# Four passes over blocks of 256 tokens become two passes over blocks of 512, with streamed weights

## The chip, the cores and the metric

The kernel runs on one core of a Trainium2 chip. The core has a TensorE (PE in the profile) with its own memory for sums (PSUM, eight banks of 512 fp32 columns), VectorE (DVE), ScalarE (ACT), GpSimd (POOL), and a sync engine (SP) whose queue issues nearly all DMA transfers here. Every engine takes its instructions in the order of its own queue and waits by semaphores for the others. The metric is the device time of one execution in microseconds; each time is the median of several runs.

## The reference

One layer on 2048 tokens of width 1024, fp32. One input projection gives sixteen groups of columns; three head groups work on them, and an output projection with a residual and a final RMSNorm ends the layer.

```python
hn = rmsnorm(x, norm_g)
z = jnp.einsum('bsd,de->bse', hn, w_in)
(aq, ak, av, ag, mq, mk, mv, mo, mi, mf, mg, gq, gk, gv, ga, gg) = jnp.split(z, split_idx, axis=-1)
y_a = band_chunk_attention(aq, ak, av, rel_bias) * jax.nn.silu(ag)
qk = jax.nn.silu(causal_conv(jnp.concatenate([mq, mk], axis=-1), conv_w))
h_ml = mlstm_chunkwise(mq_c, mk_c, mv, mi + b_i, mf + b_f)
y_b = jax.nn.sigmoid(mo) * head_rmsnorm(h_ml, ml_norm_g, ML_HEADS) * jax.nn.silu(mg)
h_gla = gla_chunkwise(gq, gk, gv, log_alpha)
y_c = head_rmsnorm(h_gla, gla_norm_g, GLA_HEADS) * jax.nn.silu(gg)
y = jnp.concatenate([y_a, y_b, y_c], axis=-1)
return rmsnorm(x + jnp.einsum('bse,ed->bsd', y, w_out), final_g)
```

Attention looks back 8 chunks of 64 tokens. mLSTM and GLA carry a state from chunk to chunk; both are computed in chunks of 128 or 64 tokens with a matrix inside the chunk and a state between chunks.

## The kernel before

Projections keep near fp32 precision in three matmuls: weights and activations are each split into a high and a low part of a rounded type (`load_w` L84, `load_x` L117), and `mm3` (L101 to L104) adds high x high, high x low and low x high over eight k tiles into one PSUM bank. `proj_f` gives [columns x tokens] with 256 tokens as the moving side; `proj_t` gives [tokens x columns] with up to 384 columns.

The tokens come in eight blocks of 256 (ST), and the program walks over them four times:

- Pass 1 (from L135): normalise a block (`prep` L171; the first block starts on unnormalised x, `first_step` L202), store the normalised block to DRAM (`x_d`, L195), the gates of mLSTM (`gates`), the projections mq, mk, mv with the causal convolution (`proj1` L306), and two chunks of 128 tokens of mLSTM (`mlstm` L361).
- Pass 2: reload the block from `x_d` and split it again (L123, L124), GLA with its projections (`proj2`, `gla`), and mLSTM's output gates (`proj_ml`).
- Pass 3: reload again, the projections of attention (`proj3` L696), scores and softmax (`scores`, L770 to L783), and the weighting of the values (`mix`, L805 to L827).
- Pass 4: output projection, residual and final norm (L843 on).

Each of the eleven tiles of input weights [1024 x 384] is loaded and split once. Between stages, results go through DRAM.

A chunk of mLSTM runs so. `gates` writes the rows of the stabiliser to DRAM (`nm_d` L293, `iw_d` L294). Four DMAs read them back, copied to all partitions (`nmb` L369, `iwb` L371). POOL adds the row term (L386) and masks (L387), ACT takes the exponential (L389), DVE multiplies by the scores (L392), TensorE sums over the chunk (L404) and updates the state (L410). For the head norm ACT squares (L422), DVE and POOL make a scale (L424 to L433), DVE applies it (L435), TensorE transposes (L440) and ACT writes out (L443, stored by L444).

The order on each engine is set when the program is built, by a scheduler that weighs the program's order, priorities and a model of the durations; pools of few buffers add waits. Once built, each engine's order is fixed.

Of the kernel before, what the change touches and what calls it, by code (L numbers as in the profile page):

```python
# [18 lines left out]
KT = D // P  # L19
ST = 256  # L20
L = 128
AH, MH, GH = 6, 6, 4
WT = 384
EPS = 1e-6
NEG = -1e30

# [6 lines left out]
def trunk_kernel(ctx: ExitStack, tc: tile.TileContext, xT, x, w_tiles, w_gates, w_out, norm_g, conv_w,  # L33
                 gate_sel, one_row, bias, ml_g, gla_g, final_g, out, dbg=None):
    nc = tc.nc
    S = x.shape[0]
    NS = S // ST
# [3 lines left out]
    wring = ctx.enter_context(tc.tile_pool(name="wring", bufs=4))  # L41
    raws = ctx.enter_context(tc.tile_pool(name="raws", bufs=3))
    xs = ctx.enter_context(tc.tile_pool(name="xs", bufs=2))
    zz = ctx.enter_context(tc.tile_pool(name="zz", bufs=2))
# [3 lines left out]
    def bank(tag):  # L48
        return ps_g.tile([P, 512], FP32, name=tag)

    x_d = dram.tile([NS, P, KT, ST], FP32, name="x_d")
    nm_d = dram.tile([MH, S], FP32, name="nm_d")
    iw_d = dram.tile([MH, S], FP32, name="iw_d")
    ls_d = dram.tile([P, S], FP32, name="ls_d")
    hb_d = dram.tile([P, 3, S], FP32, name="hb_d")
# [3 lines left out]
    y_d = dram.tile([NS, P, KT, ST], FP32, name="y_d")  # L59

    def z_tile(shape, dt=FP32):
        return zz.tile(shape, dt, name="z")

    def t_tile(shape, dt=FP32):
        return zz.tile(shape, dt, name="t", bufs=4)

    def u_tile(shape, dt=FP32):
        return zz.tile(shape, dt, name="u", bufs=3)
# [10 lines left out]
    ng = const.tile([P, KT], FP32, name="ng")  # L79
    cw = const.tile([P, 6, 4], FP32, name="cw")  # L80

    W = {}

    def load_w(name, src, width=WT, split=nc.gpsimd, pre=None, post=None):  # L84
        hi = wring.tile([P, KT, WT], FR, name="wh")
        lo = wring.tile([P, KT, WT], FR, name="wl")
        W[name] = (hi, lo)
        for g in range(4):
            if pre is not None:
                pre(g)  # L90
            raw = raws.tile([P, 2, WT], FP32, name="raw")
            nc.sync.dma_start(raw[:, :, :width], src[g])
            ks = slice(2 * g, 2 * g + 2)
            nc.scalar.copy(hi[:, ks, :width], raw[:, :, :width])
            split.tensor_tensor(lo[:, ks, :width], raw[:, :, :width], f32(hi[:, ks, :width]), op=ALU.subtract)  # L95
            if post is not None:
                post(g)

    def mm3(ps, kk, hi, lo, xh, xl, stat_w, first, last):
        a = (hi, lo) if stat_w else (xh, xl)  # L100
        b = (xh, xl) if stat_w else (hi, lo)  # L101
        nc.tensor.matmul(ps, a[0], b[0], start=first, stop=False)  # L102
        nc.tensor.matmul(ps, a[0], b[1], start=False, stop=False)  # L103
        nc.tensor.matmul(ps, a[1], b[0], start=False, stop=last)  # L104

    def proj_f(ps, wn, c0, X):
        hi, lo = W[wn]
        for k in range(KT):
            mm3(ps, k, hi[:, k, c0:c0 + P], lo[:, k, c0:c0 + P], X[:, k, 0, :], X[:, k, 1, :], True, k == 0, k == KT - 1)

    def proj_t(ps, wn, c0, n, X, tt):
        hi, lo = W[wn]
        t = slice(tt * P, (tt + 1) * P)
        for k in range(KT):
            mm3(ps, k, hi[:, k, c0:c0 + n], lo[:, k, c0:c0 + n], X[:, k, 0, t], X[:, k, 1, t], False, k == 0, k == KT - 1)

    def load_x(s, src, eng):  # L117
        X = xs.tile([P, KT, 2, ST], FR, name="x")
        for k0, kn in ((0, 3), (3, 3), (6, 2)):
            ks = slice(k0, k0 + kn)  # L120
            raw = raws.tile([P, 3, ST], FP32, name="raw")
            nc.sync.dma_start(raw[:, :kn], src[s, :, ks])
            nc.scalar.copy(X[:, ks, 0, :], raw[:, :kn])  # L123
            eng.tensor_tensor(X[:, ks, 1, :], raw[:, :kn], f32(X[:, ks, 0, :]), op=ALU.subtract)  # L124
        return X

    def store_y(s, k, t0, y):
        nc.sync.dma_start(y_d[s, :, k, t0:t0 + y.shape[-1]], y)

# [1 line left out]
    with ExitStack() as p1:  # L131
        big = p1.enter_context(tc.tile_pool(name="p1big", bufs=2))
        one = p1.enter_context(tc.tile_pool(name="p1one", bufs=1))

# [3 lines left out]
        rst = one.tile([MH, ST], FP32, name="rst")  # L138
        nc.vector.memset(rst, 1.0)
        for c in range(ST // L):  # L140
            nc.vector.memset(rst[:, c * L:c * L + 1], 0.0)
# [3 lines left out]
        mlg = one.tile([P, 3], FP32, name="mlg")  # L145

        def load_consts():
# [7 lines left out]
        def rstd(rb, rs):  # L155
            nc.gpsimd.tensor_tensor(rs, rs, mhalf[:, 0:2], op=ALU.pow)
            dg = one.tile([P, 2, P], FP32, name="dg", bufs=1)
            for tt in range(2):
                nc.vector.tensor_scalar(dg[:, tt, :], ident, rs[:, tt:tt + 1], None, op0=ALU.mult)
            nc.tensor.matmul(rb[:, 0:ST], ones, dg.rearrange("p a t -> p (a t)"), start=True, stop=True)  # L160

        def gate_rows(rows):
            gp = bank("w")
            for k in range(KT):
                nc.tensor.matmul(gp[32 * (k % 4):32 * (k % 4) + 32, :ST], wg[:, k, :], rows(k),
                                 start=(k < 4), stop=(k >= 4), skip_group_check=True)
            g1 = big.tile([P, ST], FP32, name="g1", bufs=1)
            nc.scalar.activation(g1, gp[:, :ST], AF.Identity, bias=onerow)
            return g1

        def prep(s):  # L171
            t0 = s * ST
            s4 = big.tile([P, 2, 2], FP32, name="s4")
            rs = big.tile([P, 2], FP32, name="rs")
            rb = bank("w")
            X = xs.tile([P, KT, 2, ST], FR, name="x")
            for tt in range(2):
                for g in range(2):
                    xt = big.tile([P, D // 2], FP32, name="xt")
                    nc.sync.dma_start(xt, x[t0 + tt * P:t0 + (tt + 1) * P, g * 512:(g + 1) * 512])  # L180
                    nc.scalar.activation(X[:, 2 * tt + g].rearrange("p l t -> p (l t)"), xt, AF.Square,
                                         accum_out=s4[:, tt, g:g + 1])
            nc.vector.tensor_tensor(rs, s4[:, :, 0], s4[:, :, 1], op=ALU.add)
            nc.vector.tensor_scalar(rs, rs, 1.0 / D, EPS, op0=ALU.mult, op1=ALU.add)
            rstd(rb, rs)
            rws = []
            for k0, kn in ((0, 3), (3, 3), (6, 2)):
                ks = slice(k0, k0 + kn)
                raw = raws.tile([P, 3, ST], FP32, name="raw")
                rws.append(raw)  # L190
                nc.sync.dma_start(raw[:, :kn], xT[:, ks, t0:t0 + ST])
                for k in range(kn):
                    nc.vector.scalar_tensor_tensor(raw[:, k, :], raw[:, k, :], ng[:, k0 + k:k0 + k + 1], rb[:, :ST],
                                                   op0=ALU.mult, op1=ALU.mult)
                nc.sync.dma_start(x_d[s, :, ks], raw[:, :kn])  # L195
                nc.scalar.copy(X[:, ks, 0, :], raw[:, :kn])
                nc.gpsimd.tensor_tensor(X[:, ks, 1, :], raw[:, :kn], f32(X[:, ks, 0, :]), op=ALU.subtract)  # L197
            g1 = gate_rows(lambda k: rws[k // 3][:, k % 3, :])
            return X, g1

        # the first step's projections start on unnormalised x, scaled as they leave PSUM
        def first_step():  # L202
            za = wring.tile([P, KT, WT], FR, name="wh")
            zb = wring.tile([P, KT, WT], FR, name="wl")
            flat = lambda t: t.rearrange("p k n -> p (k n)")
            xr = f32(flat(za))[:, 0:KT * ST].rearrange("p (k t) -> p k t", k=KT)
            sq = f32(flat(zb))[:, 0:KT * ST].rearrange("p (k t) -> p k t", k=KT)
            rbs = f32(flat(zb))[:, KT * ST:(KT + 1) * ST]
            X = xs.tile([P, KT, 2, ST], FR, name="x")
# [238 lines left out]
        for s in range(NS):  # L448
# [13 lines left out]
            if s == 0:  # L462
                unit[3]()
# [487 lines left out]
```

## Time and profile before

| | |
|---|---|
| runs | 1487.28, 1487.93, 1492.49 us, median 1487.93 |
| profiled execution | span 1480.4 us from first to last instruction; the median of the runs is 7.5 us longer |
| matmuls | 10244, TensorE busy 92% |
| DMA | 181.73 MB, 123 GB/s |

"PE" is busy from a matmul's issue to its modelled end; two matmuls in a row overlap, so a busy share of 100% is not the peak rate, and the distance of two starts is what counts. "PEclk" is the granted clock, 1.00 at full speed. "A <- B" in a row of waits reads: A sat idle until B released it; then the total, how often, and the longest, in us. In the timeline, SPq is SP's queue, which issues DMAs.

### The profile page before, as it was taken

The page shows a single profiled execution, that of the slowest core. Times are in us where ns is not written, and L with a number is a line of the kernel's source. Part 1 is how long each engine was busy: PE and PEld are TensorE (multiplying, and loading weights), DVE is VectorE, ACT ScalarE, POOL GpSimd, SP SyncE. Part 2 cuts the span into 40 slices and gives each one's busy share as a digit, 9 for nine tenths or more (in the row PEclk, how much of TensorE's full clock was granted, in tenths as well). Part 3 has the DMA queues.
Part 4 walks back from the last instruction along what each step waited for, and adds up shares of the span by engine and source line. Part 5 has one row for each costly group of instructions (what it writes and reads, how often), then busy time and mean ns, then how long its engine had stood idle before and what let it go on. Part 6 is the DMA issues. An engine that isn't in the chain of part 4 may idle for free.

```text
span 1480.4 us, 27383 instructions
## 1 busy us (share of the span) xinstructions
PE 1358.9 (92%) x10244; PEld 1276.4 (86%) x10244; DVE 702.8 (47%) x1913; ACT 566.9 (38%) x1249; POOL 589.5 (40%) x880
## 2 busy tenths in 40 slices
PE   9766787696688999999999999999999999999998
PEld 7666687685677988888898899999999999899998
DVE  7464445464457524433442433446556455554232
ACT  4444244244345312212221334445445446445232
POOL 4242433332522566545534773221322216427342
PEclk9878997898889999999999999999999999999999
DMA  7442533432526111111110467556657758935421
GB/s 227 106 113 73 101 98 74 94 96 60 117 63 181 50 47 54 58 30 47 54 61 27 132 177 210 163 151 208 183 162 201 191 160 236 312 102 192 153 86 58
DMA packets 168756, 181.73 MB, mean 123 GB/s; under 512 B 14416, under 2 KB 134832, under 8 KB 168496
## 3 DMA queue, kind: packets, MB, share of 16 engines
q1 hardware_dynamic: 164016, 171.59, 41.8%
q10 hardware_dynamic: 4608, 8.39, 1.5%
q8 instruction: 81, 1.33, 0.4%
q14 instruction: 51, 0.42, 0.1%
HBM read 131.60 MB, written 48.33 MB: 122 GB/s over the span
## 4 chain that ended last, share of the span: by engine, by line
PE 64%; DMA 18%; DVE 5%; issue 4%; POOL 4%; ACT 3%; SPq 1%; POOLq 0%; DVEq 0%; ACTq 0%
PE ip L103 16%; PE ip L102 16%; PE ip L104 16%; DMA nmb<-nm_d 6%; DMA x_d<-raw 4%; PE s L770 3%; PE tp L805 3%; PE w L597 3%; PE w L813 2%; DMA raw<-in_w_tiles 2%; DMA v_d<-v 2%; PE w L816 2%; DMA xt<-in_x 1%; PE s L608 1%; DVE z L335 1%
## 5 line engine op out<-in xcount | busy, mean ns | idle before, releaser
L103 PE MATMUL ip<-x,wh 128*128 128x256 f32 x1584 | 461.3, 291 | 6.6 <-POOL x L197 6.6
L102 PE MATMUL ip<-x,wh 128*128 128x256 f32 x1584 | 464.3, 293 | 1.6 <-issue 1.0
L104 PE MATMUL ip<-x,wl 128*128 128x256 f32 x1584 | 462.2, 292 | 0.5 <-DVE wl L95 0.5
L103 PEld LDWEIGHTS ip<-x,wh 128*128 128x128 f32 x1584 | 308.2, 195 | 17.4 <-issue 9.4
L102 PEld LDWEIGHTS ip<-x,wh 128*128 128x128 f32 x1584 | 308.4, 195 | 10.9 <-issue 7.8
L104 PEld LDWEIGHTS ip<-x,wl 128*128 128x128 f32 x1584 | 307.9, 194 | 10.0 <-issue 7.9
L102 PE MATMUL ip<-wh,x 128*128 128x384 f32 (+1 forms) x768 | 251.5, 327 | 16.7 <-ACT u L325 15.8
L103 PE MATMUL ip<-wl,x 128*128 128x384 f32 (+1 forms) x768 | 251.1, 327 | 0.0
L104 PE MATMUL ip<-wh,x 128*128 128x384 f32 (+1 forms) x768 | 250.0, 326 | 0.0
L102 PEld LDWEIGHTS ip<-wh,x 128*128 128x128 f32 x768 | 148.9, 194 | 18.9 <-ACT u L325 16.6
L783 POOL TENSOR_SCALAR pt<-pt,sm 128x640 f32<-128x640 f32 (+2 forms) x96 | 70.4, 735 | 228.3 <-DVE sm L782 199.6
L103 PEld LDWEIGHTS ip<-wl,x 128*128 128x128 f32 x768 | 149.0, 194 | 2.1 <-issue 1.9
L104 PEld LDWEIGHTS ip<-wh,x 128*128 128x128 f32 x768 | 148.9, 194 | 0.9 <-issue 0.8
L124 POOL TENSOR_TENSOR x<-raw,x 128x768 fp32r<-128x768 f32 (+1 forms) x45 | 74.9, 1691 | 68.8 <-ACT x L123 65.9
L781 ACT ACTIVATE pt<-pt,sm 128x640 f32<-128x640 f32 (+2 forms) x96 | 73.4, 764 | 60.6 <-DVE sm L778 57.5
L811 DVE TENSOR_TENSOR t<-tp,t 128x512 fp32r<-128x512 f32 (+2 forms) x126 | 74.5, 598 | 29.3 <-ACT t L810 28.7
L810 ACT CAST t<-tp 128x512 fp32r<-128x512 f32 (+2 forms) x126 | 63.7, 515 | 61.0 <-PE tp L805 54.5
L335 DVE SCALAR_TENSOR_TENSOR z<-u,cw,z 128x256 f32<-128x256 f32 x144 | 77.9, 591 | 15.9 <-ACT z L333 15.6
L770 PE MATMUL s<-kk,qq 128*128 128x256 f32 (+2 forms) x360 | 83.4, 314 | 1.5 <-DVE sm L778 1.3
L805 PE MATMUL tp<-ident,pt 128*128 128x128 f32 x420 | 74.8, 273 | 0.0
L386 POOL TENSOR_TENSOR nmb<-nmb,rt 128x768 f32<-128x768 f32 x16 | 24.7, 1544 | 125.5 <-DMA nmb<-nm_d 115.9
L594 POOL TENSOR_TENSOR prd<-gk,z 128x16 f32<-128x16 f32 (+15 forms) x128 | 63.8, 499 | 16.1 <-PE w L597 7.6
(232 smaller groups left out, 2192.0 us busy)
## 6 DMA issues: line engine op xcount, KB each, us to landing
raw<-in_w_tiles SPq DMA_DIRECT2D x44, 384.0 KB
kk<-k_d SPq DMA_DIRECT2D x36, 384.0 KB
vv<-v_d SPq DMA_DIRECT2D x36, 384.0 KB
raw<-x_d SPq DMA_DIRECT2D x32, 384.0 KB
qq<-q_d SPq DMA_DIRECT2D x96, 128.0 KB
xt<-in_x SPq DMA_DIRECT2D x28, 256.0 KB
nmb<-nm_d SPq DMA_DIRECT2D x32, 192.0 KB
q_d<-u SPq DMA_DIRECT2D x24, 256.0 KB
```

The lines of the kernel that those rows point to most:

```text
L102: nc.tensor.matmul(ps, a[0], b[0], start=first, stop=False)
L103: nc.tensor.matmul(ps, a[0], b[1], start=False, stop=False)
L104: nc.tensor.matmul(ps, a[1], b[0], start=False, stop=last)
L124: eng.tensor_tensor(X[:, ks, 1, :], raw[:, :kn], f32(X[:, ks, 0, :]), op=ALU.subtract)
L335: nc.vector.scalar_tensor_tensor(acc[:, j, :], zb[:, j, i:i + ST], cw[:, b, i:i + 1], acc[:, j, :], op0=ALU.mult, op1=ALU.add)
L594: nc.gpsimd.tensor_tensor(b16(prd[:, c % 8, :])[:, :, 0:c + 1], b16(gk)[:, :, 0:c + 1], b16(q)[:, :, c:c + 1].broadcast_to([P, NB, c + 1]) ...
L770: nc.tensor.matmul(sp[:, :cn], qq[:, l, tt * P:(tt + 1) * P], kk[:, ko + c0:ko + c0 + cn], start=(l == 0), stop=(l == 1))
L781: nc.scalar.activation(pt[:, :n], pt[:, :n], AF.Exp, bias=init, scale=-1.0, accum_out=sm[:, 2:3])
L783: nc.gpsimd.tensor_scalar(pt[:, :n], pt[:, :n], sm[:, 3:4], 0.5, op0=ALU.mult, op1=ALU.mult)
L805: nc.tensor.transpose(out=tp[:, w + x_ * P:w + (x_ + 1) * P], in_=pt[:, (b - b0) * P:(b - b0 + 1) * P], identity=ident)
L810: nc.scalar.copy(ph[:, :wd], tp[:, :wd])
L811: nc.vector.tensor_tensor(pl[:, :wd], tp[:, :wd], f32(ph[:, :wd]), op=ALU.subtract)
```

## The change

The kernel after has two passes over four blocks of 512 tokens (QT).

- Pass A makes, for a block, all input projections, mLSTM (four chunks of 128) and GLA (two halves of 256). The normalised block stays in eight tiles on chip (`prep_a`, `prep_b`); `x_d` is gone, and so is the start on unnormalised x.
- Weights are streamed: 33 tiles of 512 KB per block, each loaded, cast and split when it is needed (`load_w`, five buffers, two for the raw data, issued with raised priority). The low part alternates between POOL and DVE.
- Projections have 512 moving columns in one bank of PSUM (two banks in turn), 3936 instructions for 7104.
- Attention's gate and the outputs of mLSTM and GLA go through DRAM (`ga_d`, `o_d`).
- Pass B is attention of a block of 512 queries, then the output projection of the block before it; w_out is loaded whole after the first block's attention.

mLSTM's chunk keeps its instructions; its lines are now nmb L319, iwb L321, POOL L336 and L337, ACT L339, TensorE L354, ACT L372, POOL L379 to L383, DVE L385, TensorE L390.

```diff
-ST = 256
+QT = 512
+AHEAD = 1500
+        wring = pa_.enter_context(tc.tile_pool(name="wring", bufs=5))
+        wraws = pa_.enter_context(tc.tile_pool(name="wraws", bufs=2))
+        xs = pa_.enter_context(tc.tile_pool(name="xs", bufs=8))
+        xraws = pa_.enter_context(tc.tile_pool(name="xraws", bufs=3))
...
-    def load_w(name, src, width=WT, split=nc.gpsimd, pre=None, post=None):
-        hi = wring.tile([P, KT, WT], FR, name="wh")
-        lo = wring.tile([P, KT, WT], FR, name="wl")
...
+        def load_w(src, k):
+            w = wring.tile([P, 2 * D], FR, name="w").rearrange("p (k l n) -> p k l n", k=k, l=2)
+            with tc.high_priority(offset=AHEAD):
+                raw = wraws.tile([P, D], FP32, name="wraw")
+                nc.sync.dma_start(raw, src)
+                rv = raw.rearrange("p (k n) -> p k n", k=k)
+                nc.scalar.copy(w[:, :, 0, :], rv)
+                other().tensor_tensor(w[:, :, 1, :], rv, f32(w[:, :, 0, :]), op=ALU.subtract)
+            return w
+
+        def proj_f(name, X):
+            w = load_w(w_f[_F.index(name)], KT)
+            ps = acc_bank()
+            for k in range(KT):
+                nc.tensor.matmul(ps, w[:, k, 0, :], X[k][:, 0, :], start=(k == 0), stop=False)
+                nc.tensor.matmul(ps, w[:, k, 0, :], X[k][:, 1, :], start=False, stop=False)
+                nc.tensor.matmul(ps, w[:, k, 1, :], X[k][:, 0, :], start=False, stop=(k == KT - 1))
+            return ps
+
+        def proj_t(j, X, evac):
+            ws = [load_w(w_t[j, g], 2) for g in range(4)]
...
-                nc.sync.dma_start(x_d[s, :, ks], raw[:, :kn])
...
+        for q in range(NQ):
+            with tc.high_priority(offset=AHEAD):
+                ls, rt = gates(q, g1)
+            qk, vs, vg = proj_m(q, X)
+            mlstm(q, qk, vs, rt)
+            z = proj_g(q, X, vg)
+            if q + 1 < NQ:
+                with tc.high_priority(offset=AHEAD):
+                    rbs = prep_a(q + 1)
+            for sub in range(2):
+                gla(q, sub, z, vg, ls)
+            proj_a(q, X)
+            proj_o(q, X)
+            if q + 1 < NQ:
+                with tc.high_priority(offset=AHEAD):
+                    X, g1 = prep_b(q + 1, rbs)
...
-            Y = load_x(s, y_d, nc.gpsimd)
...
+        attention(0)
+        load_wo()
+        for q in range(1, NQ):
+            attention(q)
+            outp(q - 1)
+        outp(NQ - 1)
```

How the order moves is shown at three places.

SP's queue at a block's start. Before, the step that begins with the stores of nm_d and iw_d (L293, L294) loads one chunk's rows (nmb, iwb), then stores and loads x, and the second chunk's nmb comes four loads later:

```order
L293 DMA nm_d_79<-bc_1627 6x256
L294 DMA iw_d_80<-gi_1623 6x256
L369 DMA nmb_2147<-nm_d_79 128x3x128 x2
L371 DMA iwb_2148<-iw_d_80 64x3x128 x2
L195 DMA x_d_78<-raw_1826 128x768
L195 DMA x_d_78<-raw_1834 128x768
L195 DMA x_d_78<-raw_1842 128x512
L191 DMA raw_2324<-in_xT 128x3x256
L369 DMA nmb_2224<-nm_d_79 128x3x128 x2
```

Now, at the start of the second block, right behind the store of nm_d, the loads of nmb and iwb of two chunks (numbers 2700 and 2777, 2701 and 2778) and then the weight tiles (wraw):

```order
L319 DMA nmb_2700<-nm_d_69 128x3x128 x2
L269 DMA iw_d_70<-g_2271 6x512
L319 DMA nmb_2777<-nm_d_69 128x3x128 x2
L560 DMA y_d_76<-u_2143 128x512
L321 DMA iwb_2701<-iw_d_70 64x3x128
L560 DMA y_d_76<-u_2180 128x512
L321 DMA iwb_2701<-iw_d_70 64x3x128
L321 DMA iwb_2778<-iw_d_70 64x3x128 x2
L162 DMA wraw_2584<-in_w_t 128x1024
L162 DMA wraw_3009<-in_w_t 128x1024
L162 DMA wraw_3014<-in_w_t 128x1024
```

The loads of the second chunk moved up to those of the first, and the weights of the next projections stand behind all of them.

ACT's queue at the same place. Before, the exponentials L389 of a step's two chunks, one copy of a pair of conv projections out of PSUM (L325) between them:

```order
L443 ACTIVATE t_2219<-tp_2215,mlg_129 128x128 x3
L422 ACTIVATE t_2277<-s_2254 128x384
L389 ACTIVATE nmb_2645<-nmb_2645 128x768
L325 COPY u_2424<-ip_2425 128x2x256
L333 ACTIVATE z_2359<-u_2424,cw_112 128x256 x2
L389 ACTIVATE nmb_2722<-nmb_2722 128x768
L338 ACTIVATE th_2485<-z_2359 128x512
L325 COPY u_2488<-ip_2489 128x2x256
L333 ACTIVATE z_2359<-u_2488,cw_112 128x256 x2
```

Now, the exponentials L339 of the first two chunks, with the copies L285 of the conv projections (six per block, of which this row's u_2429 is the third) and the casts of weights L164:

```order
L296 ACTIVATE e_2355<-qk_2315 128x512
L292 ACTIVATE qk_2315<-u_2388,cw_120 128x512
L339 ACTIVATE nmb_2700<-nmb_2700 128x768
L339 ACTIVATE nmb_2777<-nmb_2777 128x768
L296 ACTIVATE e_2396<-qk_2315 128x512
L205 COPY g_3241<-pw_3239 128x512
L164 CAST w_2573<-wraw_2574 128x2x512
L285 COPY u_2429<-ip_2404 128x512
L292 ACTIVATE qk_2315<-u_2429,cw_120 128x512
L164 CAST w_2578<-wraw_2579 128x2x512
L285 COPY u_2470<-ip_2445 128x512
L296 ACTIVATE e_2437<-qk_2315 128x512
```

Both exponentials stand together, ahead of the third to sixth copy out of PSUM and of the weight casts.

POOL's queue in the middle of a block. Before, the addition L386 to a chunk's rows (nmb_2147) with the first step of the chain L429 to L433 of the chunk two before (sm_1704):

```order
L197 TENSOR_TENSOR x_1806<-raw_1826,x_1806 128x3x256
L329 COPY u_1926<-tail_1362 128x2x3
L330 COPY tail_1860<-u_1862 128x6
L386 TENSOR_TENSOR nmb_2147<-nmb_2147,rt_1646 128x768
L429 TENSOR_TENSOR sm_1704<-sm_1704 128x6
L197 TENSOR_TENSOR x_1806<-raw_1834,x_1806 128x3x256
```

Now, the addition L336 to the third chunk's rows (nmb_2854) and the chain L379 to L383 of the first chunk (sm_2755):

```order
L165 TENSOR_TENSOR w_3023<-wraw_3024,w_3023 128x2x512
L305 MEMSET v_4576 128x6
L336 TENSOR_TENSOR nmb_2854<-nmb_2854,rt_2312 128x768
L379 TENSOR_TENSOR sm_2755<-sm_2755 128x6
L337 AFFINE_SELECT nmb_2854<-nmb_2854 128x768
L380 TENSOR_TENSOR sm_2755<-sm_2755 128x6
L381 TENSOR_SCALAR sm_2755<-sm_2755 128x6
L382 TENSOR_TENSOR sm_2755<-sm_2755,mhalf_99 128x6
L383 TENSOR_TENSOR sm_2755<-sm_2755 128x6
L347 TENSOR_TENSOR t_2805<-qk_2315,iwb_2778 128x384
```

In both the addition that needs the loaded rows stands ahead of a chain of the chunk two before; now that is the third chunk of a block against its first, inside one block of projections.

More of the change, by code (lines that the diff above doesn't have):

```diff
@@ L99, in mm3 @@
[L99 to L125, printed above, removed]
@@ L259, in trunk_kernel @@
[L259 to L269 removed]
+            nc.sync.dma_start(glg, gla_g)
@@ L292, in gates @@
[L292 to L300 removed]
+                nc.scalar.activation(rows[32:32 + MH, cs], rows[0:MH, cs], AF.Exp, bias=nm[:, (c + 1) * L - 1:(c + 1) * L])
@@ new lines, in gates @@
+            ml = big.tile([MH, 1], FP32, name="ml")
+            nc.vector.tensor_copy(ml, mr[:, QT - 1:QT])
+            st["m"] = ml
+            nc.sync.dma_start(nm_d[:, t0:t0 + QT], nm)
+            nc.sync.dma_start(iw_d[:, t0:t0 + QT], iw)
+            rt_ps = prep_bank()
+            for c in range(NC):
+                nc.tensor.transpose(out=rt_ps[:, c * P:c * P + 96], in_=rows[0:96, c * L:(c + 1) * L], identity=ident[:96, :96])
+            rt = big.tile([P, NC, 3, 2, 3], FP32, name="rt")
@@ L364, in mlstm @@
+            proj_t(0, X, evac)
+            return qk, vs, vg
+        def mlstm(q, qk, vs, rt):
+            for c in range(NC):
+                t0 = q * QT + c * L
                 cs = slice(c * L, (c + 1) * L)
@@ L680, in trunk_kernel @@
+    with ExitStack() as pb_:
+        big = pb_.enter_context(tc.tile_pool(name="bbig", bufs=2))
+        one = pb_.enter_context(tc.tile_pool(name="bone", bufs=1))
+        wo = one.tile([P, KT, 2, D], FR, name="wo")
         bt = one.tile([P, AH, 256], FP32, name="bt")
```

897 lines of the change are left out of this document (374 added, 523 removed).

## The prediction

> **What bounds the kernel now.** I read the page's share of busy time and the granted clock first, then a table of windows that puts one row on each of the four passes (their ends are read from the lines in the timeline), then the waits.
>
> ```profile
> span 1480.4 us, 27383 instructions
> PE 1358.9 (92%) x10244; PEld 1276.4 (86%) x10244; DVE 702.8 (47%) x1913; ACT 566.9 (38%) x1249; POOL 589.5 (40%) x880
> PEclk9878997898889999999999999999999999999999
> ```
>
> ```profile
> core 0: us, PE busy (x) PEld busy (x) DVE busy (x) ACT busy (x) POOL busy (x), PEclk, DMA share, GB/s
> 0.00:462.00 462.00, 354.11 (x2464) 320.00 (x2465) 248.83 (x592) 188.19 (x374) 158.53 (x229) 0.86 0.43 104
> 462.00:862.00 400.00, 399.41 (x3245) 354.80 (x3245) 165.71 (x450) 104.62 (x238) 206.50 (x434) 1.00 0.21 63
> 862.00:1325.00 463.00, 456.52 (x3572) 453.16 (x3572) 239.68 (x763) 223.44 (x505) 157.41 (x155) 1.00 0.68 195
> 1325.00:1480.00 155.00, 148.89 (x968) 148.44 (x966) 48.57 (x111) 50.68 (x133) 67.09 (x63) 1.00 0.35 117
> ```
>
> The two tables say one thing: TensorE is the bound from 462 us on, at full clock and with almost no gap, and only pass 1 (mLSTM) has slack: 462 - 354 = 108 us without a matmul. In it the clock is 0.86 as well, so (1 - 0.86) x 354 = about 49 us of the busy time is half-speed loss. Passes 3 and 4 lose 6.5 + 6.1 = 12.6 us. So the **dense** TensorE work is about 1480 - 108 - 49 - 13 = 1310 us. What opens the holes in pass 1 is in the waits, and one hole is shown by the timeline and the chain (the shorter stalls add up to the rest):
>
> ```profile
> POOL nmb L386 <- DMA nmb<-nm_d: 115.9, 13, 15.3
> ACT nmb L389 <- POOL nmb L387: 91.5, 11, 16.9
> DVE t L435 <- POOL sm L433: 77.1, 8, 16.4
> PE tp L440 <- DVE t L435: 62.3, 8, 14.0
> ```
>
> ```profile
> 110.45 12.83 DMA nmb<-nm_d
> ...
> 163.12 15.65 DMA nmb<-nm_d
> ```
>
> ```profile
> 109.97 0.96 SPq L369 DMA_DIRECT2D nmb<-nm_d  x2
> 111.03 0.43 SPq L191 DMA_DIRECT2D raw<-in_xT  x1
> ...
> 161.18 1.24 SPq L371 DMA_DIRECT2D iwb<-iw_d  x2
> 162.53 1.07 SPq L369 DMA_DIRECT2D nmb<-nm_d  x2
> ```
>
> ```profile
> 123.44 1.47 POOL L386 TENSOR_TENSOR nmb<-nmb,rt 128x768 f32<-128x768 f32 x1 [12.71 <-DMA nmb<-nm_d]
> 128.38 0.90 PE L440 MATMUL tp<-ident,t 128*128 128x128 f32 x3 [11.25 <-DVE t L435]
> ```
>
> The two loads that copy a gate row to all partitions (L369) take 12.8 us to land. POOL stands at L386 for them, and the short statistics of the previous chunk (L429 to L433) stand behind it in POOL's queue; DVE L435 needs these, TensorE's transposes L440 need DVE, and all later projections are queued behind L440. Two loads alone take 12.8 us; with two half as large (L371, 64 partitions) put ahead of them they take from 161.2 to 178.8 us, 17.6 us. So I read the loads as **serial**: 6.1 us for each L369, about 3 for each L371. After such a hole the clock is down:
>
> ```profile
> 126.00:128.40 2.40, 0.03 (x1) 0.50 0.00 0
> 128.40:131.40 3.00, 3.00 (x12) 0.50 0.59 175
> 131.40:134.00 2.60, 2.60 (x13) 0.50 0.64 173
> 134.00:137.00 3.00, 3.00 (x29) 0.99 0.44 135
> ```
>
> 5.6 us at half clock after it, 12 or 13 matmuls in a stretch that holds 29 later, so each hole costs some 3 us (half of 5.6) more than its length. The Trainium skill ("TensorE: Matmul & The Clock Gate", What's actually happening) says that the array falls to half clock after an idle window of about 3.4 us and needs one busy window to come back; the trace agrees here, with 0.50 for 5.6 us and then 0.99.
>
> **The change part by part.** *Wider projections.* Their pitch is the distance of starts in a dense stretch, not the duration printed (0.28 to 0.34 us is latency):
>
> ```profile
> 1298.37 0.34 PE L103 MATMUL ip<-wl,x 128*128 128x384 f32 x1
> 1298.54 0.34 PE L104 MATMUL ip<-wh,x 128*128 128x384 f32 x1
> 1298.72 0.34 PE L102 MATMUL ip<-wh,x 128*128 128x384 f32 x1
> ...
> 1304.08 0.28 PE L102 MATMUL ip<-wh,x 128*128 128x256 f32 x1
> 1304.20 0.28 PE L103 MATMUL ip<-wl,x 128*128 128x256 f32 x1
> 1304.32 0.28 PE L104 MATMUL ip<-wh,x 128*128 128x256 f32 x1
> ```
>
> 0.174 us for 384 columns, 0.120 for 256. The program has 5568 of 256 and 1536 of 384 columns: 668 + 267 = 935 us. Along the same line 512 columns take 0.174 + 0.054 = 0.228 us (an estimate), and there are 3936: 897 us. Saved 38 us; bounds 0 (no fixed part) to 86 (0.216 us, were the whole 13 ns of fixed part gone). Attention, mLSTM and GLA keep their matmuls. Dense after: 1310 - 38 = **1272 us**.
>
> *Normalised x kept on chip, no round trip.* This takes away 72 casts L123 and 72 subtractions L124, nearly all in passes 2 to 4, where the windows show TensorE at 399 of 400 us: worth nothing. The three stores L195 per step leave the queue of pass 1 too, but the streamed weights take their place.
>
> *Streamed weights.* 132 tiles of 512 KB, 69 MB instead of 17 MB. Pass 3 moved 195 GB/s while TensorE was 456.5 of 463 us busy; one tile per 24 projections (5.5 us) is 95 GB/s. The casts:
>
> ```profile
> L94 ACT CAST wh<-raw 128x768 fp32r<-128x768 f32 x52 | 42.3, 830 | 51.2 <-DMA raw<-in_w_tiles 46.1 <-DMA raw<-in_w_out 3.4 <-PE ip L103 1.3
> L95 POOL TENSOR_TENSOR wl<-raw,wh 128x768 fp32r<-128x768 f32 x24 | 44.6, 1879 | 16.8 <-ACT wh L94 16.6
> ```
>
> scaled to 1024 columns, 1.1 us on ACT and 2.5 us on POOL (DVE takes every other one) per 5.5 us of projection. On average they hide; where POOL or ACT stand in a wait, the ring of five tiles is what is left. I charge it inside the stall term.
>
> *Start.* Before, matmuls run almost from the first microseconds, on x not yet normalised:
>
> ```profile
> 0.00:37.00 37.00, 33.61 (x222) 27.88 (x222) 27.65 (x49) 18.43 (x33) 16.53 (x24) 1.00 0.73 227
> ```
>
> Now nothing is projected until four tiles of x are squared and summed, the scale is spread, and x is loaded again, scaled and split. At the 227 GB/s of this row the 4 MB of x alone take 18 us, and the chain ends with DVE and ACT work, some 10 us: 28 us against the 3 us of idle in this row, **+25** (10 to 35).
>
> *Pass B.* Attention no longer has the attention projections beside it, only the output projection of the block before.
>
> ```profile
> L710 DVE SCALAR_TENSOR_TENSOR u<-ip,u 128x256 fp32r<-128x256 f32 x48 | 20.3, 422 | 17.0 <-ACT u L709 15.2 <-DMA v_d<-v 0.7
> L770 PE MATMUL s<-kk,qq 128*128 128x256 f32 (+2 forms) x360 | 83.4, 314 | 1.5 <-DVE sm L778 1.3
> L805 PE MATMUL tp<-ident,pt 128*128 128x128 f32 x420 | 74.8, 273 | 0.0
> L813 PE MATMUL w<-t,vv 128*128 128x256 f32 (+1 forms) x252 | 51.2, 284 | 4.4 <-DMA vv<-v_d 2.9 <-ACT t L810 1.5
> L816 PE MATMUL w<-t,vv 128*64 128x256 f32 (+1 forms) x252 | 47.1, 269 | 0.0
> ```
>
> In pass 3 DVE works 240 us by its window; without L710 and the like of the projections some 220 are attention's. Attention's 1284 matmuls, at 0.11 us each (the pitch of the widths between 128 and 384), are about 141 us; the output projection is 768 x 0.228 = 175. Fully interleaved, B is 316, and 20 more in the first block, which has nothing beside it (half as wide a band: DVE 40 against TensorE's 20): 336. One after the other it is 220 + 175 = 395, and 400 with its ends. The middle, 369, is **+53** over the dense time (20 to 85). At the boundary the last output-gate tile waits for GLA's result by way of DRAM, and q, k, v loads queue behind it: **+18** (10 to 25).
>
> *mLSTM's stalls move, they do not go.* Chunk loads and POOL chain are the same lines (L319 to L390). What is new is that one block issues the loads of **two** chunks together (4 x 6.1 + 4 x 3 = 36 us of queue), and weight tiles stand behind them in SP's queue. By ACT's order both exponentials L339 stand ahead of the third evacuation of the conv projections; with two PSUM banks TensorE gets two tiles (11 us) past the second. The second chunk's row lands 25 us after issue, POOL adds 2 x (1.5 + 0.9), ACT 1.7: about 31 us from the loads on, of which 11 are covered: 20 us of hole, for three blocks; 10 in the first, whose evacuations stand ahead. With 3 us of clock each, 70 + 12 = 82 us. In mid-block POOL takes L336 of the third chunk before L379 to L383 of the first: from L354 to L390 that is 18 to 20 us as now, and TensorE's order leaves 47 to 54 projections, 11 to 12 us. Two holes of 7 us and 2.5 of clock per block: 76 us. Another 22 for weight tiles late behind the loads and for X passed on at block ends. **Stalls 180 us** (60 to 260; 60 is one 12 us hole with its clock per block, 260 is every chunk at the 16 us that the waits give as longest).
>
> **Sum**: 1272 + 25 + 53 + 18 + 180 = 1548 us of span. The median of the three runs is 7.5 us above the profiled span of before, so 1555 us, 4.5% slower. In one sentence: 170 us of stalls and clock (108 + 49 + 13) become 180, and 38 us of matmul are won against 96 of new idle.
>
> As to the pitch, the Trainium skill (same page, Back-to-back issue gap) gives N/2.4 + 2.5 ns for an isolated matmul and 131 ns sustained at N = 512. At 256 columns the first gives 109 ns where the trace shows 120, and no row shows anything like the second; by the first the sum would be some 48 us less.
>
> **Rivals.** (1) *The cover works*, faster: the block has 180 us of projections, and if TensorE meets at each chunk enough of them, only the first hole of a block is left, 12 + 3 us: stalls 60, time 1435. For it: pass 2, where GLA's chain hides whole. Against it: an in-order queue, where the holes come from what stands next, not from what exists. It decides at 1480 - 1368 = 112 us of stalls, 28 per block. (2) *The loads of different tiles overlap* and the burst takes 13 us, not 25: 60 us of the block-start holes go, 1495, no change. For: 16 DMA engines; against: 17.6 us when four stood together. (3) *Weights become the bound* after each burst, since the fourth weight tile comes behind 36 us of queue with a ring of five: another 20 us per block, 1635. (4) *512-column matmuls flow better than the line through 256 and 384* and TensorE's dense time drops by 100 us or more: 1455 or less. The page's 131 ns would be 3936 x 0.131 = 516 us of projections, and about 1175. (5) The output projection interleaves fully and the start is short: 1555 - 33 - 15 = 1507, still slower.
>
> **How the numbers follow.** Forecast with (5), 1500 to 1610: 0.60. Rival 1: 0.14. Rival 2: 0.11, split on both sides of no change. Rival 3: 0.13. Rival 4: 0.02. About 0.5% is what a measurement of this kernel can tell from no change (1480 to 1495). Faster: rivals 1 and 4 and a little of 2, 0.18; same 0.07; slower 0.75. The range is 1455 to 1635: it takes in rival 2, the near half of 1 and 3, and leaves about 0.1 out at each end.
>
> **What would show it.** In the changed profile: dense starts of projections 0.228 us apart; a first projection at about 28 us; four groups of TensorE holes of some 20 us at the block starts whose releaser is PSUM's evacuation, behind ACT L339, behind POOL, behind the loads L319; holes of 5 to 9 us before L390; a clock under 1 in the first half of each block and at 1 in the second. Wrong would be: loads that land in 12 us though four are queued, no wait at L390, projections at 0.216 us or less apart, or pass B at 340 us or at 400.

## The result and the profile after

The changed kernel takes 1616.99 us (median of 4 runs, 1611.55 to 1618.31) against 1487.61 us: ratio 1.0856, 95% interval 1.0829 to 1.0883. It is slower by 8.6%; the forecast was 4.5% (1555 us, range 1455 to 1635).

The page of the changed kernel, its first lines and the clock:

```profile
span 1616.6 us, 20006 instructions
PE 1384.3 (86%) x6924; PEld 1074.4 (66%) x6924; DVE 722.3 (45%) x1653; ACT 628.1 (39%) x1235; POOL 692.4 (43%) x897
PEclk7999999879989998898999789999957999999989
```

TensorE idles for 1616.6 - 1384.3 = 232 us, against 122 before. The half clock comes on top. The clock of a row is a mean over time, and idle time at half clock counts in it (the prediction's row 126.00:128.40 has 0.50 with 0.03 us of work), so it can't be multiplied by the busy time. Laid over each other, the trace's half-clock stretches and TensorE's busy time share 124 us here and 79 before; half of that, 62 and 39 us, is lost. What is left, the dense work, is 1322 us here (1616.6 less 232.3 and 62.2) and 1319 before (1480.4 less 121.5 and 39.4). So everything lost is idle time and half clock, and what the wider projections gave is gone again inside the dense work (see below). A table of windows (start, pass A, the passage to pass B, the first block of attention, the rest) shows where:

```profile
core 0: us, PE busy (x) PEld busy (x) DVE busy (x) ACT busy (x) POOL busy (x), PEclk, DMA share, GB/s
0.00:50.00 50.00, 28.65 (x97) 16.07 (x98) 23.66 (x55) 22.86 (x35) 22.36 (x30) 0.82 0.71 227
50.00:1169.00 1119.00, 986.98 (x4768) 744.48 (x4769) 466.28 (x874) 388.41 (x712) 480.85 (x672) 0.93 0.40 109
1169.00:1192.00 23.00, 2.21 (x13) 1.70 (x13) 1.01 (x3) 1.01 (x3) 7.80 (x10) 0.57 0.56 142
1192.00:1254.00 62.00, 44.09 (x223) 37.93 (x223) 37.68 (x151) 39.20 (x94) 36.58 (x39) 0.69 0.95 261
1254.00:1616.00 362.00, 322.38 (x1829) 274.23 (x1827) 193.69 (x571) 176.60 (x393) 144.82 (x149) 0.96 0.50 148
```

Idle plus half clock, row by row: 21 + 3 at the start; 132 + 34 in pass A; 21 + 1 in the passage; 18 + 14 in the first block of attention; 40 + 10 in the rest. With the 1322 us of dense work this is the span.

The waits in pass A that answer to those of before:

```profile
POOL nmb L336 <- DMA nmb<-nm_d: 155.3, 15, 15.1
ACT nmb L339 <- POOL nmb L337: 124.2, 10, 18.7
PE ip L172 <- ACT u L285: 40.0, 6, 16.6
PE ip L172 <- ACT zg L410: 30.1, 4, 10.1
PE tp L390 <- DVE t L385: 20.1, 4, 6.9
```

POOL waits for the gate rows as before, and longer. TensorE's holes have moved: only 20 us now stand before the transposes (62 before), and 70 us stand before projections, which wait for a PSUM bank to be emptied. One block start in order of time, from the timelines of SP, POOL, ACT and PE (start, duration, and in brackets the idle time before and its releaser):

```profile
323.52 1.09 SPq L319 DMA_DIRECT2D nmb<-nm_d  x2
325.57 0.90 SPq L319 DMA_DIRECT2D nmb<-nm_d  x2
326.68 3.90 SPq L560 DMA_DIRECT2D y_d<-u  x1
```

```profile
335.56 1.47 POOL L336 TENSOR_TENSOR nmb<-nmb,rt 128x768 f32<-128x768 f32 x1 [7.36 <-DMA nmb<-nm_d]
346.98 1.47 POOL L336 TENSOR_TENSOR nmb<-nmb,rt 128x768 f32<-128x768 f32 x1 [9.95 <-DMA nmb<-nm_d]
```

```profile
347.62 0.58 ACT L285 COPY u<-ip 128x512 f32<-128x512 f32 x1 [19.96 <-DMA y_d<-u]
348.25 0.79 PE L172 MATMUL ip<-x,w 128*128 128x512 f32 x1 [12.36 <-ACT u L285]
```

The first chunk's rows are there 12 us after the first load's issue, the second's 23.5 us after the same moment. Here the evacuation L285 was held not by the exponential ahead of it but by a store: its buffer u was still to be written out by L560, and that store stood in the queue behind the four loads. In the next two blocks the exponentials come first on ACT, as forecast:

```profile
647.97 1.66 ACT L339 ACTIVATE nmb<-nmb 128x768 f32<-128x768 f32 x2 [18.71 <-POOL nmb L337]
...
651.47 0.58 ACT L285 COPY u<-ip 128x512 f32<-128x512 f32 x1
651.60 1.91 PE L220 MATMUL pw<-xraw,wg 128*32 128x512 f32 x2 [13.96 <-DVE xraw L217]
...
929.28 0.84 ACT L339 ACTIVATE nmb<-nmb 128x768 f32<-128x768 f32 x1 [17.59 <-POOL nmb L337]
...
935.49 0.57 ACT L285 COPY u<-ip 128x512 f32<-128x512 f32 x1
936.11 0.79 PE L172 MATMUL ip<-x,w 128*128 128x512 f32 x1 [16.65 <-ACT u L285]
```

In both, ACT waits some 18 us for POOL. In the fourth block (at 936 us) TensorE then waits for the evacuation behind the exponentials. In the third (at 652 us) its hole ends with a matmul of the gates, L220: DVE scales the x for it (L217) behind an operation (L297) that waits for ACT L296, and this stands behind the exponentials. In mid-block a weight tile is caught in the same way, behind the loads of the fourth chunk:

```profile
442.87 14.14 DMA wraw<-in_w_f
...
458.68 0.79 PE L172 MATMUL ip<-x,w 128*128 128x512 f32 x1 [10.07 <-ACT zg L410]
```

512 KB of weights took 14.1 us from issue (the median of such tiles is 3.7 us), and TensorE lost 10 us: the evacuation L410 stands on ACT behind the cast of this tile and, in this block, behind an exponential that waits for its rows until 452.4 us. Such a hole, 5 to 10 us, stands in each of the four blocks, 30 us in all.

### The profile page after: what moved, and what is told of

It reads as the page before. It is cut to its first block, busy times and chain, and to the rows that moved or that the text cites. A ratio compares the mean times of both kernels' runs of the same rounds, so it can differ in the third digit from the quotient of the medians.

```text
span 1616.6 us, 20006 instructions
## 1 busy us (share of the span) xinstructions
PE 1384.3 (86%) x6924; PEld 1074.4 (66%) x6924; DVE 722.3 (45%) x1653; ACT 628.1 (39%) x1235; POOL 692.4 (43%) x897
## 4 chain that ended last, share of the span: by engine, by line
PE 59%; DMA 22%; DVE 5%; ACT 5%; issue 4%; POOL 4%; SPq 1%; POOLq 0%; ACTq 0%; DVEq 0%
PE ip L172 9%; PE ip L173 9%; PE ip L174 9%; DMA nmb<-nm_d 6%; DMA wraw<-in_w_f 5%; PE ip L728 3%; PE ip L730 3%; PE ip L729 3%; PE w L454 2%; DMA raw<-y_d 2%; PE ip L184 2%; PE s L633 2%; PE ip L185 2%; PE ip L186 2%; DMA y_d<-cc 2%
## 5 line engine op out<-in xcount | busy, mean ns | idle before, releaser
L172 PE MATMUL ip<-x,w 128*128 128x512 f32 x800 | 329.5, 413 | 70.2 <-ACT u L285 40.0
L173 PE MATMUL ip<-x,w 128*128 128x512 f32 x800 | 328.1, 410 | 0.0
L174 PE MATMUL ip<-x,w 128*128 128x512 f32 x800 | 324.3, 405 | 0.0
L165 POOL TENSOR_TENSOR w<-wraw,w 128x1024 fp32r<-128x1024 f32 x66 | 159.4, 2416 | 272.0 <-ACT w L164 272.0
L164 ACT CAST w<-wraw 128x1024 fp32r<-128x1024 f32 x132 | 138.5, 1049 | 270.2 <-PE ip L174 145.6
L172 PEld LDWEIGHTS ip<-x,w 128*128 128x128 f32 x800 | 155.5, 195 | 122.0 <-ACT u L285 42.4
L173 PEld LDWEIGHTS ip<-x,w 128*128 128x128 f32 x800 | 155.7, 195 | 42.1 <-issue 11.7
L174 PEld LDWEIGHTS ip<-x,w 128*128 128x128 f32 x800 | 155.0, 194 | 41.9 <-issue 10.6
L165 DVE TENSOR_TENSOR w<-wraw,w 128x1024 fp32r<-128x1024 f32 x66 | 88.9, 1347 | 183.0 <-ACT w L164 182.9
L728 PE MATMUL ip<-wo,y 128*128 128x512 f32 x256 | 105.1, 411 | 26.6 <-ACT y L715 26.0
L633 PE MATMUL s<-kk,qq 128*128 128x256 f32 (+2 forms) x360 | 87.7, 347 | 33.3 <-DMA vv<-v_d 18.1
L184 PE MATMUL ip<-w,x 128*128 128x512 f32 x256 | 103.5, 405 | 1.0 <-ACT vg L306 1.0
L729 PE MATMUL ip<-wo,y 128*128 128x512 f32 x256 | 103.6, 405 | 0.0
L730 PE MATMUL ip<-wo,y 128*128 128x512 f32 x256 | 102.3, 407 | 0.2 <-POOL y L716 0.2
L185 PE MATMUL ip<-w,x 128*128 128x512 f32 x256 | 102.1, 400 | 0.0
L186 PE MATMUL ip<-w,x 128*128 128x512 f32 x256 | 101.1, 397 | 0.0
L633 PEld LDWEIGHTS s<-kk,qq 128*128 128x128 f32 x360 | 62.6, 213 | 42.9 <-issue 20.9
L336 POOL TENSOR_TENSOR nmb<-nmb,rt 128x768 f32<-128x768 f32 x16 | 23.5, 1468 | 155.3 <-DMA nmb<-nm_d 155.3
```

The lines of the kernel that those rows point to most:

```text
L164: nc.scalar.copy(w[:, :, 0, :], rv)
L165: other().tensor_tensor(w[:, :, 1, :], rv, f32(w[:, :, 0, :]), op=ALU.subtract)
L172: nc.tensor.matmul(ps, w[:, k, 0, :], X[k][:, 0, :], start=(k == 0), stop=False)
L173: nc.tensor.matmul(ps, w[:, k, 0, :], X[k][:, 1, :], start=False, stop=False)
L174: nc.tensor.matmul(ps, w[:, k, 1, :], X[k][:, 0, :], start=False, stop=(k == KT - 1))
L184: nc.tensor.matmul(ps, X[k][:, 0, t], w[:, 0, :], start=(k == 0), stop=False)
```

## The experiments

The theory: the loads that give one row to all partitions are slow and one after the other, and set the stalls of pass A. Its rivals: the streamed weights, or the order of the merged pass, set them. The first four experiments are single runs, on a chip where the kernel before took 1481 us and not 1488; the others were repeated. So a saving against the changed kernel has two figures: by the ratios to the kernel before on the same chip (1.0856 for the change), and by the difference of the times.

**Own rows.** Every partition reads a row of its own; count, size and wait of the loads stay. The stabiliser's values are left out.

```diff
-    nc.sync.dma_start(nmb[:, 3 * b:3 * b + 3, :],
-                      nm_d[:, t0:t0 + L].rearrange("(a b) t -> b a t", b=2)[b].partition_broadcast(P))
+    nc.sync.dma_start(nmb[:, 3 * b:3 * b + 3, :], nm_w[:, 3 * b:3 * b + 3, c * L:c * L + L])
...
+    nc.sync.dma_start(nm_w[0], nm)
```

> The changed kernel, with every partition reading its own row of a DRAM tile (filled once, and written in one row by the gates, so that the wait on the gates stays) in place of all partitions reading the same row: same number of loads, bytes and 512-byte pieces; the stabiliser's values are left out. Theory (loads of one row by all partitions are slow and serial in SP's queue, and set the stalls of pass A): the loads land in 3 to 5 us, POOL's wait at L336 falls from 155 us to under 50, the holes at the block starts and before L390 go, time 1460 to 1530. Rival (the streamed weights with two raw buffers, or the order of the merged pass, set the stalls): within 25 us of 1617.

1505.6 us, 102 to 111 us less. The table of DMA issues gives the median from issue to landing, here and in the changed kernel:

```profile
nmb<-nm_w SPq DMA_DIRECT2D x32, 192.0 KB, 3.2
nmb<-nm_d SPq DMA_DIRECT2D x32, 192.0 KB, 11.2
```

Apart from filling the new tiles at the start, nothing else differs but the place that is read. The theory holds; weights and order, which are as before, are out as the main cause.

**Long pieces.** A chunk's three rows lie side by side in DRAM, so each partition reads one piece of 1536 bytes. The values loaded are the same.

```diff
-    nm_d = dram.tile([MH, S], FP32, name="nm_d")
+    nm_d = dram.tile([S // L, 2, 3 * L], FP32, name="nm_d")
...
-            nc.sync.dma_start(nm_d[:, t0:t0 + QT], nm)
+            for b in range(2):
+                nc.sync.dma_start(nm_d[t0 // L:(t0 + QT) // L, b].rearrange("c (a t) -> a c t", t=L),
+                                  nm[b:MH:2].rearrange("a (c t) -> a c t", t=L))
...
+                    nc.sync.dma_start(nmb[:, 3 * b:3 * b + 3, :].rearrange("p a t -> p (a t)"),
+                                      nm_d[t0 // L, b].partition_broadcast(P))
```

> The changed kernel with the gate rows of a chunk stored side by side in DRAM, so that a partition's copy is one piece of 1536 bytes and not three of 512; same bytes, same results. If the price of the loads is per piece: L319's two loads land in 4 to 5 us and not 12, time 1470 to 1540. If it is per byte read from the same place: 1600 to 1620. Rival (weights or order): 1600 to 1620 too, with landing in 4 to 5 us.

1506.5 us, 101 to 110 us less. The same block start as above, and the wait of the whole run:

```profile
315.43 0.35 SPq L323 DMA_DIRECT2D nmb<-nm_d  x1
319.67 0.61 SPq L323 DMA_DIRECT2D nmb<-nm_d  x1
```

```profile
324.81 1.69 POOL L340 TENSOR_TENSOR nmb<-nmb,rt 128x768 f32<-128x768 f32 x1 [0.18 <-DMA nmb<-nm_d]
```

```profile
POOL nmb L340 <- DMA nmb<-nm_d: 27.9, 8, 8.5
```

The second chunk's rows are in use 9.4 us after the first load's issue, not 23.5, though the bytes are the same: the price is one of pieces. In pass A no hole before L172 is left that a weight tile or a store caused; what remains above 3.2 us there stands where one block ends and the next begins (7 to 10 us): the transposes of GLA's last output wait for its norm on DVE, those of the gates for ACT, or a projection waits for the first evacuation of the new block, which stands behind the gates on ACT.

**Loads from POOL's queue.** They take as long to land (11.5 us, median), but nothing stands behind them in SP's queue.

```diff
-                    nc.sync.dma_start(nmb[:, 3 * b:3 * b + 3, :],
+                    nc.gpsimd.dma_start(nmb[:, 3 * b:3 * b + 3, :],
```

> The changed kernel with the loads of nmb and iwb issued by POOL, not by SP, so that weights and stores no longer stand behind them in SP's queue. Theory: the holes before projections that wait for a weight tile (5 to 10 us, one per block) and the evacuations that wait for a store of y go; those that wait for the rows themselves stay: 1530 to 1590. Rival (what stands behind in the queue does not matter, and POOL pays for issuing): 1615 to 1670.

1585.7 us. Of the 101 to 110 us, 22 to 31 come back by freeing SP's queue; this shows the direction, though not that it is all queueing, since POOL also issues in another order. The holes did not all go as expected: evacuations in mid-block (L410, L411) still hold TensorE up for 16 us, where it was 30.

**Rows copied by TensorE.** Twelve matmuls of 128 columns per chunk in place of the loads.

```diff
+    nc.tensor.matmul(pn[:, j * L:(j + 1) * L], ident[0:MH, hh:hh + 1].broadcast_to([MH, P]), st["nw"][0:MH, cs],
+                     start=True, stop=True)
...
+    nc.vector.tensor_tensor(nmb[:, h0:h0 + hn, :], pn[:, 0:hn * L].rearrange("p (a t) -> p a t", t=L),
+                            rt[:, c, 0, h0:h0 + hn].unsqueeze(2).broadcast_to([P, hn, L]), op=ALU.add)
```

> The changed kernel with the rows copied to all partitions by TensorE (12 matmuls of 128 columns per chunk against one-hot columns), evacuated by DVE (with the addition of L336) and ACT; no loads of nmb and iwb at all. Theory: no wait for rows; TensorE pays about 40 us for the 192 matmuls, stalls of pass A fall from some 200 us to under 80: 1500 to 1550. Rival (weights or order): 1640 to 1670.

1549.4 us, 58 to 68 us less than the change though TensorE does more: a third way without the slow loads that is faster, at the upper end of the expectation.

**The same edit in the kernel before.** Long pieces, there in blocks of 256.

> The kernel before, with the one edit of e2: the gate rows of a chunk side by side in DRAM, one piece of 1536 bytes per partition. Theory (the same loads make the holes of pass 1, 108 us without a matmul and 49 us of half clock): POOL's wait at L386 nearly goes, pass 1 shrinks by 80 to 120 us, time 1370 to 1410, so that the change with the same edit (1506) is slower still by 100 us or more, by its start, its pass B and its block ends. Rival (the long loads were a burden of the changed order alone, and pass 1's holes come from its short blocks): 1450 or more, and both kernels are within 60 us once edited.

1383.6 us (1381.74 to 1383.87), ratio 0.9351 to the kernel before (0.9329 to 0.9373). This version beats both kernels. The first three passes, and POOL's wait:

```profile
0.00:395.00 395.00, 370.17 (x2748) 332.05 (x2749) 283.84 (x638) 201.12 (x398) 168.44 (x243) 0.97 0.43 134
395.00:790.00 395.00, 393.17 (x3185) 348.02 (x3184) 152.22 (x421) 100.91 (x231) 221.59 (x438) 1.00 0.23 68
790.00:1225.00 435.00, 429.26 (x3352) 425.94 (x3351) 232.32 (x744) 214.03 (x487) 135.24 (x137) 1.00 0.67 193
```

```profile
L390 POOL TENSOR_TENSOR nmb<-nmb,rt 128x768 f32<-128x768 f32 x16 | 24.4, 1527 | 36.8 <-DMA nmb<-nm_d 7.9 <-DVE z L339 7.5 <-DVE raw L193 6.7
```

Pass 1 shrank from 462 to some 395 us; its idle time is 25 us and its clock 0.97 where it had been 108 us and 0.86. Thus the slow loads cost 96 us before the change (1480.0 on this chip) and 101 to 110 us after it, and with them mended in both, the change still costs 1506.5 - 1383.6 = 123 us. The rest asks where these come from.

**The output projection between the heads.** In the change with long pieces, the four tiles of a block's output projection are put between the heads of the next attention.

```diff
+                if q and 1 <= h <= NC:
+                    out_tile(q - 1, h - 1, Y)
```

> e2 with the four token tiles of a block's output projection put between the heads of the next block's attention, where they stood behind all heads. Theory (pass B loses 90 us because attention alone is bound by DVE and POOL while TensorE idles or is at half clock): pass B 428 us falls to 370 to 400, time 1460 to 1485. Rival (the scheduler had interleaved them as far as buffers allow, and pass B waits for its loads and stores): 1500 to 1515.

1512.2 us (1507.38 to 1514.1): a miss. The first matmul of the output projection starts some 60 us after the first score in both; after that, stretches of 20 us hold projections and scores mixed in both. The scheduler had mixed them already.

**w_out later.** Its load is written into the second block's attention.

```diff
+                if q == 1 and h == 2:
+                    load_wo()
```

> e2 with the load and split of w_out moved from behind the first block's attention into the second block's. Theory (pass B starts with some 80 us in which 4 MB of w_out fill the DMA queue and ACT and POOL, ahead of the keys and values of attention: 22 us without a matmul and 14 us of half clock there): 12 to 30 us less than e2's 1506, that is 1475 to 1495. Rival (the first block's attention is bound by its own chain through DVE, ACT and POOL, with nothing beside it): 1500 to 1512.

1503.7 us (1499.19 to 1506.1), which decides nothing, since the loads did not move. The table of DMA issues for the first 77 us of pass B has seven of the eight tiles:

```profile
raw<-in_w_o SPq DMA_DIRECT2D x7, 512.0 KB
```

**One tile of w_out.** Seven tiles of the output weights are left out.

```diff
-            for g in range(KT):
+            for g in range(1):
...
-                        nc.tensor.matmul(ps, Y[k][:, 0, t], wo[:, k, 0, c], start=(k == 0), stop=False)
+                        nc.tensor.matmul(ps, Y[k][:, 0, t], wo[:, 0, 0, c], start=(k == 0), stop=False)
```

> e2 with one of the eight tiles of w_out loaded and split, and used for all eight (seven tiles of the output weights are left out), since in e9 the queue took seven of the eight loads into the same stretch all the same. Theory (w_out's 4 MB and its casts hold up the first attention block): the first 80 us of pass B shrink by 15 to 30 us, time 1475 to 1492. Rival (that block is bound by its own chain and by the loads of keys and values): 1498 to 1510.

1493.4 us (1490.5 to 1494.89), 13 us less than 1506, just short of what the theory forecast and more than its rival allows. From the first score to the first matmul of the output projection it is 49.9 us, against 62.0 with all tiles. So w_out holds up the first block by 12 us. The other 50 us, whose matmuls would fill 20 by the prediction's estimate, stay: attention's chain through DVE, ACT and POOL or its loads of keys and values, with the DMA engines 0.93 busy from 1075 to 1110 us in this run. Which of the two was not tried.

**No norm in the first block.** Its scale is set to one, so the first 512 tokens are left unnormalised.

```diff
-        rbs = prep_a(0)
+        rbs = g_tile([P, QT])
+        nc.vector.memset(rbs, 1.0)
```

> e2 without the norm of the first block (its scale is set to one, so the first 512 tokens are left unnormalised): the squares, the power and the spreading matmul of that block are left out. Theory (the start costs what stands before the first projection): TensorE's first projections come 12 to 16 us earlier and the time falls by 10 to 18 us. Rival (the start is bound by loading x and the first weights, which stay): less than 5 us.

1486.3 us (1485.28 to 1491.07), 20 us less. The first 50 us of this run and of the change with long pieces:

```profile
0.00:50.00 50.00, 45.24 (x167) 30.01 (x168) 35.49 (x67) 30.67 (x44) 26.14 (x34) 0.97 0.67 226
...
0.00:50.00 50.00, 32.22 (x102) 18.69 (x103) 24.20 (x56) 24.83 (x38) 23.68 (x31) 0.81 0.73 236
```

The projections flow from 15 us on, not from 32 us: the start costs what stands ahead of the first projection, and the loads of x hide beside it.

## Why the prediction was right, and where its sizes were off

*Wider projections: right.* The start of one 512-column matmul to the next, in a dense stretch of the changed kernel:

```profile
522.09 0.39 PE L174 MATMUL ip<-x,w 128*128 128x512 f32 x1
522.32 0.39 PE L172 MATMUL ip<-x,w 128*128 128x512 f32 x1
522.54 0.40 PE L173 MATMUL ip<-x,w 128*128 128x512 f32 x1
```

0.227 us, where 0.228 was forecast. By the mean distance of two starts (at full clock, idle time taken out) the projections fell from 7104 x 0.138 = 980 us to 3936 x 0.2396 = 943, so 37 us were won for 38. Rival 4 is out. The Trainium skill's two figures for 512 columns ("TensorE: Matmul & The Clock Gate", Back-to-back issue gap), 216 and 131 ns, are both under what this kernel shows.

*Dense work: 1322 us for 1272.* Two steps of the working were off. Its 49 us of half clock in pass 1 apply the row's mean clock to the busy time; laid over the busy time they are 36, and the dense work before was 1319 us, not 1310. And "attention, mLSTM and GLA keep their matmuls" holds for their number, not for their time, which the working left as it was: by the same mean, attention's 1284 matmuls took 0.111 us each before and take 0.128 now, 143 and 164 us, and GLA's 86 and 97. With some smaller groups that is about 40 us. Why their starts moved apart was not tried; before, attention had its projections beside it, and now it has the output projection alone.

*Serial loads: right, and the main term.* 12 and 23.5 us for the first and second chunk is what 6.1 us a load gives; rival 2 (they overlap) is out, and the two experiments that make the loads short show that they are the cause. Rival 1 (the cover works) is out with them. Rival 3 (weights as the bound) is half right: weight tiles did come late, by one hole of 5 to 10 us per block and not 20 us, but only behind these loads, and with short loads the holes go.

*Stalls of pass A: right mechanism, 166 us for 180.* Block starts had holes of 12, 14 and 17 us and not 20 each, the first block hardly any and not 10; the evacuation behind the exponentials ended the last of them, a store behind the loads the first, and the gates' matmul the second. Before L390 there was one hole per block (3 to 7 us) and not two. Against that, 22 us for late weights and block ends were too little: late weights made 30, and between blocks 25 us were lost to GLA's last norm (before L518), the gates of the next block (before L272), or the first evacuation behind them (L285). The block ends stay with short loads. The clock took 34 us, where the sum had 12 at the block starts and 20 in mid-block. That the whole came near is in part luck, since holes priced too high and too low made up for each other.

*Start and passage: right.* 25 us for 25 (the experiment gives 20 for the norm's part), and 22 us for 18.

*Pass B: the part that was mis-sized most.* It was to take 369 us, the middle between full interleaving and none, and took 425; by the prediction's own sign (400) this part was wrong. Idle time and half clock were to cost 53 us and cost 32 + 50 = 82; most of the rest are the matmuls of attention with wider distances. The step that failed in the first block is its price by DVE's busy time, 40 us with "20 more" than TensorE's: the block took 62 us with TensorE busy for 44 of them, at a clock of 0.69. Twelve of these are w_out's. In the remaining 362 us TensorE is busy for 322. Rival 5 (full interleaving, 336 us, and a short start) did not come: the scheduler had mixed projection and scores, and the pass was longer all the same. Which link of the chain through DVE, ACT and POOL, or which load, holds pass B was not tried.

Together: 50 (dense) + 0 (start) - 14 (pass A) + 4 (passage) + 29 (pass B) = 69 us, the gap between the forecast span of 1548 and 1617. The working adds 7.5 us from the span to the median; here the median was 0.4 us above the span, so the forecast time of 1555 was 62 us short.

So the direction came for the forecast reason in its larger part: the stalls stay (166 us in pass A, where idle time and half clock cost 161 in the whole kernel before), and the new idle time and half clock of start, passage and pass B are 128 us, forecast 96. But the cheaper matmuls, 38 us in the sum, gave nothing on balance. The pair of edited kernels shows it more sharply: of the 127 us by which the change is slower on their chips (8.56% of 1481), the loads account for 5 by the ratios (101 - 96), and some 122 stay without them. Where these are, the windows of the change with long pieces tell (the passage, the first block of attention, the rest with its last output projection):

```profile
1056.00:1078.00 22.00, 1.52 (x9) 1.01 (x8) 1.02 (x3) 1.01 (x3) 7.30 (x9) 0.56 0.56 144
1078.00:1160.00 82.00, 60.12 (x331) 51.43 (x331) 52.36 (x202) 51.90 (x122) 45.33 (x50) 0.76 0.91 250
1160.00:1446.00 286.00, 263.77 (x1542) 226.87 (x1540) 169.94 (x500) 151.66 (x339) 116.64 (x121) 0.96 0.53 157
1446.00:1505.00 59.00, 44.58 (x180) 35.69 (x180) 9.23 (x20) 11.99 (x26) 19.87 (x18) 0.89 0.21 76
```

Idle time and half clock, laid over the busy time as above, are 21 + 36 + 31 + 17 = 105 us; the kernel before with the same edit has some 14 in its last two passes. Start and pass A cost 76 us (22 of them at the start, some 25 at the block ends), against 37 in its first two. Less 6 us of dense work (1324 against 1329), that is 91 + 39 - 6 = 124 us, the difference of the two spans (1504.8 - 1380.0). The block ends and the later part of pass B are read from the profile, not tried.

## What to carry to other kernels

Look for the wait that ends last, and ask what the change does to *it*: here a wait for small loads bounded a stage before, and a rebuild of the whole kernel left it in place, while another layout of the rows in DRAM, a few lines, gave 6.5% to the kernel before. A load that many partitions make from one place should be cut into as few pieces as possible, and what stands behind it in the same queue (stores whose buffers are reused, weights) belongs to its price. A pass that is merged or cut off loses the work that used to lie beside its chains: count what is left for TensorE at each block end and in the first block of a pass.

## What the runs showed of the hardware

Reading one row by all partitions is slow by itself: 128 x 3 pieces of 512 bytes landed 11.2 us after issue (median) where all partitions read the same three rows, 3.2 us where each read its own, with the same count, size and queue. With 1536 bytes to a piece, the pieces from one place cost no more than those of 512 bytes did: at a block start, four loads of 384 pieces took 23.5 us, and four of 128 with three of 64 between them 9.4 us, which is 15 and 13 ns a piece. The half clock adds a quarter to a third to the idle time of TensorE here: 62 us of half-speed loss with 232 us idle in the change, 39 with 122 in the kernel before, and 12 with 39 (1380.0 - 1341.1) in the kernel before with long pieces. A mean clock over a stretch with holes says more than that, since it counts the holes: 0.921 in the change would be 109 us.
